# A two-layer decoder trunk: the low part of every second first-layer weight piece, on GpSimd or on VectorE

## The chip, the cores and the metric

The kernel runs on one core of one Trainium2 chip. The metric is the device time of one execution in microseconds (us); lower is better.

## What is computed

The input x is 512 x 1024 in float32. It passes two post-norm layers, each `x <- LayerNorm(alpha * x + sublayer(x))`. All arithmetic is meant in float32.

The first ("even") layer multiplies x by one wide input projection, whose columns feed two branches:

```python
proj = einsum('bsd,de->bse', x, w_in)      # q, k, v, g_ret, xb, g_lru, 1024 columns each
ret  = retention(rope(q), rope(k), v)      # 8 heads, decay per head, then a norm per head
ret  = ret * silu(g_ret)
lru  = rg_lru_branch(xb, ...) * silu(g_lru)   # width-4 convolution, two gates, a scan over time
y    = einsum('bse,ed->bsd', concatenate([ret, lru]), w_out)
```

The second ("odd") layer is differential attention with 8 heads, a gate path, and an output projection.

## The kernel before

**Numbers in two parts.** TensorE multiplies in a rounded 32-bit format (float32r). To keep float32 accuracy, every operand is kept as a pair: a high part, which is the operand rounded to float32r, and a low part, which is operand minus high part. A product is then three matrix products, high x high, high x low and low x high (`mm3`, lines 148 to 151). The pair is made by the helper `split` (line 139): ScalarE copies the source into the high part (line 145), and VectorE subtracts the high part from the source to give the low part (line 146). For weights that carry a scale, which occur only in the second layer, lines 142 and 143 do the same with a scale. Since `split` serves every operand, a row of the profile at L146 is told apart by its tile: `w59l` is the low part of weight piece 59, `k2l` the low part of head 2's rotated keys, `r53l` that of a block of retention scores, `retm3l` that of a finished retention branch, and so on. The letter h in place of l is the high part.

**Weight pieces.** The weights are cut on the host into pieces of 128 x 1024, in the order of their use, and numbered from 0 (list `order`). The pieces 0 to 63 belong to the first layer: 48 of its input projection and, mixed in where they are used, 16 of its output projection. From piece 64 on they belong to the second layer. `fetch` (line 163) brings the next piece: SyncE (SP) issues its DMA into a raw buffer (line 170), then `split` makes its two parts. There are two raw buffers, so the DMA of piece n+2 waits until both parts of piece n have been made. `take` (line 176) fetches so far ahead that mostly two pieces stand ready beyond the one in use.

**Order of the work.** TensorE and SP run in the order in which the program is written; for the other engines a scheduler orders the instructions by priority and by its own estimate of times, when the kernel is built. TensorE's order is a stream of projections (`t_unit`, `s_unit`, `out_unit`: 24 products of 512 columns for one weight piece) with side work between the products: class `Side` holds jobs (retention heads, recurrent channel blocks, attention blocks) that issue their next products after a given number of ticks of three products, written out by hand in the tables `RET_START`, `RET_SCORES`, `LRU_GATES` and so on. A side job's products can come only when VectorE and ScalarE have made their operands by then; otherwise TensorE waits.

**Lines that matter here.** In a retention head: rotation of q and k (lines 297 to 302), scores times decay (line 413, `rsd` from the PSUM tile `rs`), the products into `ro`, the square `rq` (line 424), its split, the mean by TensorE into `rv` (lines 430 and 431), and the norm (lines 435 to 445). In a recurrent block: the convolution `xc` in three VectorE steps (line 456), its split, the gates' products `pr` and `pi`, the steps at lines 472 to 484, whose last is the scan, and the product with the gate (line 487). The names that end in `_ps`, and `rs`, `ro`, `rv`, `pr`, `pi`, `ht`, are PSUM tiles; the others lie in SBUF. GpSimd works in the layer norm and in the second layer only, on one column at a time (`rsqrt`, lines 315 and 316, and line 591).

Of the kernel before, what the change touches and what calls it, by code (L numbers as in the profile page):

```python
# [8 lines left out]
F32 = mybir.dt.float32  # L9
F32R = mybir.dt.float32r  # L10
AF = mybir.ActivationFunctionType
ALU = mybir.AluOpType
# [11 lines left out]
LAMBDA_INIT = 0.8 - 0.6 * math.exp(-0.3)  # L24
MASKED = -3.0e38

# how many ticks the jobs' stages wait (see Side), by head, channel block or query block
RET_START = (13, 13, 13, 13, 13, 13, 13, 8)
RET_SCORES = (4, 4, 4, 7)
RET_NORM = (8, 6, 8, 6, 8, 6, 5, 5)  # L30
# [4 lines left out]
ATT_TURN = (4, 3, 4, 4)  # L35
ATT_NORM = 5
ATT_VALUE = 2
# how far the scheduler prefers these instructions to earlier ones
P_ROPE, P_SCORES, P_SQUARE, P_GROUP, P_VALUE = 50, 13, 60, 5, 60
P_CONV, P_GATES = 9, 5  # L40
P_LN, P_LAST, P_WEIGHTS, P_ATT = 10, 10, 450, 337
# [2 lines left out]


class Side:
    """Work that runs between the projections' products: jobs are generators that yield how many
    ticks (three products of 512 columns) have to pass before their next products are issued, or
    a condition for that."""

    def __init__(self):
        self.jobs = []
# [1 line left out]
        self.free = {}  # L54

    def add(self, gen, group, limit, wait=0, gap=0):
        """At most ``limit`` jobs of a group run at once, and they start ``gap`` ticks apart."""
        job = {"gen": gen, "at": self.now + wait, "group": group, "limit": limit, "gap": gap, "when": None, "started": False, "done": False}
        self.jobs.append(job)
        return job  # L60
# [35 lines left out]
def trunk(ctx: ExitStack, tc: tile.TileContext, a):  # L96
    nc = tc.nc
# [21 lines left out]
    ALL = slice(None)  # L119
# [4 lines left out]
    def temp(name):  # L124
        return es.tile([P, S], F32, tag="es", name=name)

    def bank(pl, tag, name):
        return pl.tile([P, 512], F32, tag=tag, name=name)

    def pair(pl, shape, tag, name, **kw):  # L130
        return tuple(pl.tile(shape, F32R, tag=tag + x, name=name + x, **kw) for x in "hl")

    def part(n, name):
        return pair(sp, [P, n], f"s{n}", name, bufs=2 if n == S else 1)

    def cut(t, *ix):
        return t[0][ix], t[1][ix]

    def split(src, dst, scale=None):
        if scale is not None:  # L140
            s = sg[:, scale:scale + 1]
            nc.scalar.activation(out=dst[0], in_=src, func=AF.Identity, scale=s)
            nc.vector.scalar_tensor_tensor(out=dst[1], in0=src, scalar=s, in1=dst[0].bitcast(F32), op0=ALU.mult, op1=ALU.subtract)
            return
        nc.scalar.copy(out=dst[0], in_=src)  # L145
        nc.vector.tensor_tensor(out=dst[1], in0=src, in1=dst[0].bitcast(F32), op=ALU.subtract)  # L146

    def mm3(out, l, r, start, stop):
        nc.tensor.matmul(out=out, lhsT=l[0], rhs=r[0], start=start, stop=False)  # L149
        nc.tensor.matmul(out=out, lhsT=l[0], rhs=r[1], start=False, stop=False)  # L150
        nc.tensor.matmul(out=out, lhsT=l[1], rhs=r[0], start=False, stop=stop)  # L151
# [3 lines left out]
        nc.sync.dma_start(out=t, in_=src)  # L155
        return t

    # ------------------------------------------------------------------ the weights' pieces, in the order of their use
    ew, ow, eo, oo = a["ev_w"], a["od_w"], a["ev_wo"], a["od_wo"]
    order, ready = [], []  # L160
    extra, stats = {}, {}

    def fetch():
        if len(ready) < len(order):
            n = len(ready)
            src, scale = order[n]
            raw = wraw.tile([P, D], F32, tag="raw", name=f"w{n}_r")
            w = pair(extra.pop(n, wsp), [P, D], "w", f"w{n}")
            for c in ([slice(0, HALF), slice(HALF, D)] if n == 0 else [slice(0, D)]):
                nc.sync.dma_start(out=raw[:, c], in_=src[:, c])  # L170
                split(raw[:, c], cut(w, ALL, c), scale=scale)
            ready.append(w)

    taken = [0]
# [69 lines left out]
    for p in range(3):  # L244
        one, two = (2 * p, 2 * p + 1)
# [5 lines left out]
    for kind, i in ev:  # L251
        if kind in ("ro", "lo", "out"):
            order += [(eo[2 * i + j + n], None) for n in {"ro": (0,), "lo": (8,), "out": (8, 0)}[kind] for j in range(2)]
        else:
            n = 4 if kind == "v" else 1
# [20 lines left out]
    ones = const.tile([P, P], F32R, tag="ones", name="ones")  # L276
# [60 lines left out]
        return [[load(f"{name}{r}{hf}", [P, HALF], src[r:r + 1, hf * HALF:hf * HALF + HALF].partition_broadcast(P), *next(slots))  # L337
                 for hf in range(2)] for r in range(2)]

    # ------------------------------------------------------------------ even layer  # L340
    phase = ctx.enter_context(ExitStack())
    es = pool("es", 10, phase)
    qkp = pool("qkp", 2, phase)
# [1 line left out]
    y = big.tile([P, SB, D], F32, tag="y", name="y")  # L345
# [10 lines left out]
    cos = load("cos", [P, S], a["cos"])  # L356
    sin = load("sin", [P, S], a["sin"])

    # 4 * softplus(-lambda), softplus(z) = max(z, 0) + log1p(exp(-|z|)), log1p(y) = 2 atanh(y / (2 + y))
    sp4 = const.tile([P, KT], F32, tag="sp4", name="sp4")  # L360
    sa = const.tile([P, KT], F32, tag="sa", name="sa")
    sb_ = const.tile([P, KT], F32, tag="sb_", name="sb_")
# [1 line left out]
    lam = vecs[:, 7]  # L364
# [40 lines left out]
    def retention(h, q, k, v, dec, m):  # L405
        ss = []
        for jb in range(SB):
            n = S - jb * P
            ps = bank(ps_sc, "sc", f"rs{h}{jb}")
            mm3(ps[:, :n], cut(k, ALL, slice(jb * P, jb * P + P)), cut(q, ALL, slice(jb * P, S)), True, True)  # L410
            with tc.high_priority(P_SCORES):
                s = temp(f"rsd{h}{jb}")
                nc.vector.tensor_tensor(out=s[:, :n], in0=ps[:, :n], in1=dec[:, :n], op=ALU.mult)  # L413
                t = part(n, f"r{h}{jb}")
                split(s[:, :n], t)
            ss.append(t)
            yield RET_SCORES[jb]
        ps = bank(ps_av, "av", f"ro{h}")
        hs = (h % 4) * P
        for jb in range(SB):  # L420
            mm3(ps[:, jb * P:], cut(v[jb], ALL, slice(hs, hs + P)), ss[jb], jb == 0, jb == SB - 1)
        with tc.high_priority(P_SQUARE):
            sq = temp(f"rq{h}")
            nc.scalar.activation(out=sq, in_=ps, func=AF.Square)
            t = part(S, f"rq{h}")
            split(sq, t)
        seen.add(h)
        yield RET_NORM[h]
        pv = bank(ps_tp, "tp", f"rv{h}")
        nc.tensor.matmul(out=pv, lhsT=ones, rhs=t[0], start=True, stop=False)  # L430
        nc.tensor.matmul(out=pv, lhsT=ones, rhs=t[1], start=False, stop=True)
        with tc.high_priority(P_GROUP):
            sd = temp(f"rsd{h}")
            # one Newton step makes r = exp(-ln(var + eps) / 2) exact: (r r (var + eps) - 3) r = -2 / sqrt(var + eps)
            nc.scalar.activation(out=sq, in_=pv, func=AF.Ln, bias=epsb)
            nc.scalar.activation(out=sd, in_=sq, func=AF.Exp, scale=-0.5)
            nc.scalar.activation(out=sq, in_=sd, func=AF.Square)
            nc.vector.scalar_tensor_tensor(out=sq, in0=pv, scalar=EPS, in1=sq, op0=ALU.add, op1=ALU.mult)
            nc.vector.scalar_tensor_tensor(out=sd, in0=sq, scalar=3.0, in1=sd, op0=ALU.subtract, op1=ALU.mult)
            n1 = sq  # L440
            nc.vector.tensor_tensor(out=n1, in0=ps, in1=sd, op=ALU.mult)
            nc.vector.tensor_scalar(out=n1, in0=n1, scalar1=gng[:, h:h + 1], scalar2=gn[:, 1, h:h + 1], op0=ALU.mult, op1=ALU.add)
        if ("gr", h) not in gates:
            yield lambda: ("gr", h) in gates
        nc.vector.tensor_tensor(out=n1, in0=n1, in1=gates.pop(("gr", h)), op=ALU.mult)
        split(n1, cut(m, ALL, h % 2))

    def lru(c, ps, m):
# [15 lines left out]
        t = temp(f"t{c}")  # L464
# [2 lines left out]
        mm3(pi, cut(gw[0], ALL, slice(o + P, o + 2 * P)), t2, True, True)  # L467
        i = xb
        nc.scalar.activation(out=i, in_=pi, func=AF.Sigmoid, bias=gbx(c))  # L469
        # t = tanh(-log_a / 2): a = (1 - t) / (1 + t), sqrt(1 - a^2) = 2 sqrt(t) / (1 + t)  # L470
        nc.scalar.activation(out=t, in_=t, func=AF.Tanh, scale=sp4[:, c:c + 1])
        nc.vector.tensor_tensor(out=i, in0=i, in1=xc, op=ALU.mult)  # L472
        d = xc
        r = temp(f"r{c}")
        # d = -1 / (1 + t), by one Newton step from exp(-ln(1 + t))
        nc.scalar.activation(out=r, in_=t, func=AF.Ln, bias=1.0)
        nc.scalar.activation(out=r, in_=r, func=AF.Exp, scale=-1.0)  # L477
        nc.vector.scalar_tensor_tensor(out=d, in0=t, scalar=1.0, in1=r, op0=ALU.add, op1=ALU.mult)  # L478
# [28 lines left out]
    for kind, i in ev:  # L507
# [5 lines left out]
        elif kind == "xb":  # L513
            if i % 2 == 0:
                raw = load(f"gw{i}", [P, 4 * P], a["gw"][i // 2], pl=es, tag="es")
# [42 lines left out]
    hj = []  # L558
    even_out(("lru", "ret"), 3, "eo", after=even_end)

    # ------------------------------------------------------------------ odd layer
    phase.close()
    lq = load("lq", [P, 4, P], a["lq"].partition_broadcast(P), pl=wk, tag="wk")
    nc.vector.tensor_tensor(out=lq[:, 0:2], in0=lq[:, 0:2], in1=lq[:, 2:4], op=ALU.mult)
# [6 lines left out]
    def attention(hd, qb, q, k, m):  # L571
        hc = (hd % 2) * 2 * P
        n = (qb + 1) * P
        ee = []
        z = small.tile([P, 2], F32, tag="z", name="z")
# [8 lines left out]
                nc.scalar.activation(out=e, in_=ps[:, :n], func=AF.Exp, scale=-1.0, bias=nm, accum_out=z[:, mp:mp + 1])  # L584
            ee.append(e)
        with tc.high_priority(P_ATT):
            # e0 / z0 - lam e1 / z1 = (e0 - lam (z0 / z1) e1) / z0; the RMS norm takes the 1 / z0, its epsilon times z0^2
            zr = small.tile([P, 2], F32, tag="zr", name="zr")
            nc.vector.reciprocal(out=zr[:, 0:1], in_=z[:, 1:2])  # L589
            nc.vector.tensor_scalar(out=zr[:, 0:1], in0=zr[:, 0:1], scalar1=z[:, 0:1], scalar2=nlam, op0=ALU.mult, op1=ALU.mult)  # L590
            nc.gpsimd.tensor_scalar(out=zr[:, 1:2], in0=z[:, 0:1], scalar1=z[:, 0:1], scalar2=EPS, op0=ALU.mult, op1=ALU.mult)  # L591
            nc.vector.scalar_tensor_tensor(out=ee[0], in0=ee[1], scalar=zr[:, 0:1], in1=ee[0], op0=ALU.mult, op1=ALU.add)  # L592
# [171 lines left out]
```

## Time and profile before

| | before |
|---|---|
| three runs | 947.27, 947.78, 945.7 us |
| median | 947.27 us |
| span of the profiled execution, first to last instruction | 944.1 us |
| mean granted TensorE clock | 0.994 |
| busy: TensorE / VectorE / ScalarE / GpSimd | 924.1 / 692.6 / 462.2 / 55.7 us |

The profiled execution is known by its span alone; the median of the runs is 3.2 us over it. In the profile PE is TensorE's products, PEld its weight loads, DVE is VectorE, ACT is ScalarE, POOL is GpSimd, SP or SPq is SyncE's queue of DMA issues. A row of the timeline has start, length, engine, line, operation, output<-inputs and shape; in square brackets behind it stands how long the engine had been idle before and what ended that. A row of the waits has who waited for whom, the total, the number of times and the longest. A row of the groups ends in busy time, mean ns of one, and the idle time ahead of it. In the busy times by stage each engine has its busy time and its number of instructions.

### The profile page before, as it was taken

How to read it: one execution, taken by the hardware profiler on the slowest of the kernel's cores; microseconds unless marked ns; L12 is line 12 of the kernel's file. 1: busy time of each engine (PE TensorE's matmuls, PEld its weight loads, DVE VectorE, ACT ScalarE, POOL GpSimd, SP SyncE). 2: the span in 40 equal slices, each digit the busy share in tenths (PEclk: the TensorE clock that was granted, in tenths of full speed). 3: DMA queues.
4: the chain of work that ended last, by engine and by line, in shares of the span. 5: the costliest groups of instructions: out<-in, count | busy, mean ns of one | idle time of the engine just before them, and what ended most of it. 6: DMA issues, size and time to landing. Idle time of an engine off the chain costs nothing.

```text
span 944.1 us, 11558 instructions
## 1 busy us (share of the span) xinstructions
PE 924.1 (98%) x4327; PEld 764.1 (81%) x4327; DVE 692.6 (73%) x1171; ACT 462.2 (49%) x749; POOL 55.7 (6%) x117
## 2 busy tenths in 40 slices
PE   8999999999999999999999999999999999999995
PEld 6888888878888888888887888888788888887884
DVE  6777997867869988994489854478844488636687
ACT  5567786566374776423334454233453234444330
POOL 0000000000000000000001210100100001101012
PEclk9999999999999999999999999999999999999998
DMA  6462221412414123305221122042222141223102
GB/s 225 156 215 87 69 88 56 166 58 69 143 33 167 57 90 115 123 18 173 90 89 68 67 90 90 23 134 90 68 70 86 45 134 67 85 79 114 57 23 90
DMA packets 27416, 88.94 MB, mean 94 GB/s; under 512 B 3424, under 2 KB 3552, under 8 KB 27360
## 3 DMA queue, kind: packets, MB, share of 16 engines
q1 hardware_dynamic: 27360, 88.20, 27.8%
q8 instruction: 34, 0.56, 0.2%
q14 instruction: 22, 0.18, 0.1%
HBM read 86.09 MB, written 2.10 MB: 93 GB/s over the span
## 4 chain that ended last, share of the span: by engine, by line
PE 74%; DVE 13%; ACT 5%; issue 3%; POOL 2%; DMA 1%; SPq 0%; POOLq 0%; DVEq 0%; ACTq 0%
PE ov_ps L151 3%; PE ov_ps L149 3%; PE ov_ps L150 3%; PE og_ps L149 3%; PE og_ps L150 2%; PE og_ps L151 2%; PE oo_ps L149 2%; PE oo_ps L150 2%; PE oo_ps L151 2%; PE ev_ps L149 2%; PE ev_ps L151 2%; PE ev_ps L150 2%; PE xb_ps L151 1%; PE xb_ps L150 1%; PE xb_ps L149 1%
## 5 line engine op out<-in xcount | busy, mean ns | idle before, releaser
L584 ACT ACTIVATE e<-as,nm 128x128 f32<-128x128 f32 (+3 forms) x64 | 33.2, 523 | 29.1 <-DVE nm L581 28.8
L615 DVE SCALAR_TENSOR_TENSOR o<-po,ars,og 128x256 f32<-128x256 f32 x32 | 15.5, 483 | 39.9 <-POOL ars L316 39.9
L581 DVE CUSTOM_DVE_ANT_0 as<-as,mask 128x128 f32<-128x128 f32 (+3 forms) x64 | 30.1, 509 | 1.9 <-PE as L151 1.9
L591 POOL TENSOR_SCALAR zr<-z 128x1 f32<-128x1 f32 x32 | 11.2, 351 | 309.1 <-ACT e L584 309.1
L315 POOL TENSOR_SCALAR rs_t<-bmv 128x1 f32<-128x1 f32 x8 | 3.8, 469 | 430.2 <-DVE bmv L326 430.2
L611 ACT ACTIVATE po<-po 128x256 f32<-128x256 f32 x32 | 11.9, 371 | 29.8 <-PE po L151 29.8
L315 POOL TENSOR_SCALAR rs_t<-ss,zr 128x1 f32<-128x1 f32 x32 | 15.9, 496 | 140.7 <-ACT po L611 135.7
L456 DVE SCALAR_TENSOR_TENSOR xc<-xbp,vecs,xc 128x509 f32<-128x509 f32 (+2 forms) x24 | 17.8, 743 | 2.1 <-ACT xc L453 1.9
L234 DVE TENSOR_TENSOR y<-oo_ps,y 128x512 f32<-128x512 f32 x24 | 16.2, 683 | 4.2 <-PE oo_ps L151 4.2
L316 POOL TENSOR_TENSOR ars<-rs_t,nhalf 128x1 f32<-128x1 f32 x32 | 18.9, 590 | 2.7
L592 DVE SCALAR_TENSOR_TENSOR e<-e,zr,e 128x128 f32<-128x128 f32 (+3 forms) x32 | 17.6, 550 | 1.0
L589 DVE RECIPROCAL zr<-z 128x1 f32<-128x1 f32 x32 | 5.2, 162 | 15.1 <-ACT e L584 14.9
L413 DVE TENSOR_TENSOR rsd<-rs,dec 128x512 f32<-128x512 f32 (+3 forms) x32 | 15.4, 483 | 0.8 <-PE rs L151 0.7
L620 PEld LDWEIGHTS po<-ident,o 128*128 128x128 f32 x64 | 8.4, 140 | 7.7 <-DVE o L615 4.5
L620 PE MATMUL po<-ident,o 128*128 128x128 f32 x64 | 12.6, 278 | 1.5 <-DVE o L615 1.3
L596 PE MATMUL wt<-ident,e 128*128 128x128 f32 x80 | 14.0, 273 | 0.0
L596 PEld LDWEIGHTS wt<-ident,e 128*128 128x128 f32 x80 | 10.4, 140 | 3.9 <-DVE e L592 0.4
L145 ACT CAST hh<-ht 128x512 fp32r<-128x512 f32 x8 | 4.7, 588 | 17.5 <-PE ht L551 17.5
L472 DVE TENSOR_TENSOR xbp<-xbp,xc 128x512 f32<-128x512 f32 x8 | 5.5, 690 | 10.0 <-ACT xbp L469 10.0
L584 ACT ACTIVATION_READ_ACCUMULATOR e<-as,nm 128x1 f32 x64 | 12.5, 196 | 0.0
L382 ACT ACT_TABLE_LOAD x9 | 11.5, 1283 | 1.5 <-PE gl_ps L151 1.4
L478 DVE SCALAR_TENSOR_TENSOR xc<-t,r 128x512 f32<-128x512 f32 x8 | 5.5, 690 | 9.0 <-ACT r L477 9.0
(2665 smaller groups left out, 3409.9 us busy)
## 6 DMA issues: line engine op xcount, KB each, us to landing
w_r<-in_od_w SPq DMA_DIRECT2D x64, 512.0 KB, 3.3
w_r<-in_ev_w SPq DMA_DIRECT2D x47, 512.0 KB, 3.3
w_r<-in_ev_wo SPq DMA_DIRECT2D x16, 512.0 KB, 3.4
w_r<-in_od_wo SPq DMA_DIRECT2D x16, 512.0 KB, 3.3
dec<-in_dec SPq DMA_DIRECT2D x8, 256.0 KB, 3.8
y<-in_x SPq DMA_DIRECT2D x4, 512.0 KB, 6.8
out_h<-y SPq DMA_DIRECT2D x8, 256.0 KB, 2.1
xr<-in_xt SPq DMA_DIRECT2D x3, 512.0 KB, 6.7
```

The costliest lines, as they stand in the source:

```text
L149: nc.tensor.matmul(out=out, lhsT=l[0], rhs=r[0], start=start, stop=False)
L150: nc.tensor.matmul(out=out, lhsT=l[0], rhs=r[1], start=False, stop=False)
L151: nc.tensor.matmul(out=out, lhsT=l[1], rhs=r[0], start=False, stop=stop)
L234: nc.vector.tensor_tensor(out=yy, in0=ps, in1=yy, op=ALU.add)
L315: nc.gpsimd.tensor_scalar(out=t, in0=var, scalar1=scale, scalar2=eps, op0=ALU.mult, op1=ALU.add)
L316: nc.gpsimd.tensor_tensor(out=out, in0=t, in1=nhalf[:, :1], op=ALU.pow)
L456: nc.vector.scalar_tensor_tensor(out=xc[:, sh:], in0=xb[:, :S - sh], scalar=conv_w(w, c), in1=xc[:, sh:], op0=ALU.mult, op1=ALU.add)
L581: nc.vector.tensor_tensor_reduce(out=ps[:, :n], in0=ps[:, :n], in1=mask[:, S - n:], scale=-QK_SCALE, scalar=3.0e38, op0=ALU.add, op1=ALU.m ...
L584: nc.scalar.activation(out=e, in_=ps[:, :n], func=AF.Exp, scale=-1.0, bias=nm, accum_out=z[:, mp:mp + 1])
L592: nc.vector.scalar_tensor_tensor(out=ee[0], in0=ee[1], scalar=zr[:, 0:1], in1=ee[0], op0=ALU.mult, op1=ALU.add)
L596: nc.tensor.transpose(out=pt[:, kb * P:kb * P + P], in_=ee[0][:, kb * P:kb * P + P], identity=ident)
L620: nc.tensor.transpose(out=pm[:, i * P:i * P + P], in_=o[:, i * P:i * P + P], identity=ident)
```

## The change

`split` gets one more argument, the engine that makes the low part; its default is VectorE. `fetch` passes GpSimd for the pieces with an odd number from 5 to 65, and VectorE for all others. (Pieces with a scale do not look at the argument; none of them is below 66.) The high parts stay on ScalarE, the transfers on SP. The subtraction itself, with its two inputs and its result, is the same.

```diff
-    def split(src, dst, scale=None):
+    def split(src, dst, scale=None, low=nc.vector):
         if scale is not None:
...
         nc.scalar.copy(out=dst[0], in_=src)
-        nc.vector.tensor_tensor(out=dst[1], in0=src, in1=dst[0].bitcast(F32), op=ALU.subtract)
+        low.tensor_tensor(out=dst[1], in0=src, in1=dst[0].bitcast(F32), op=ALU.subtract)
...
                 nc.sync.dma_start(out=raw[:, c], in_=src[:, c])
-                split(raw[:, c], cut(w, ALL, c), scale=scale)
+                split(raw[:, c], cut(w, ALL, c), scale=scale, low=nc.gpsimd if n % 2 and 3 < n < 66 else nc.vector)
```

Beside this the diff only takes comments out; line numbers stay.

## The prediction

> **What bounds the kernel now.** I read the page first, then the busy time by stage, then who waits for whom on TensorE, then the timeline around each of those waits. Times are microseconds.
>
> ```profile
> span 944.1 us, 11558 instructions
> PE 924.1 (98%) x4327; PEld 764.1 (81%) x4327; DVE 692.6 (73%) x1171; ACT 462.2 (49%) x749; POOL 55.7 (6%) x117
> ```
>
> The whole kernel is a TensorE stream: 924.1 of 944.1. VectorE, with 73%, is no bound as an average. The change touches the first layer alone, so that stage is what counts. In the view by stage the columns are PE, PEld, DVE, ACT, POOL busy time (with counts), then granted clock and DMA.
>
> ```profile
> 26.00:386.00 360.00, 357.87 (x1620) 296.25 (x1619) 296.42 (x440) 236.03 (x310) 0.00 (x0) 1.00 0.31 105
> ```
>
> From 26 to 386 TensorE is idle for only 360 - 357.9 = 2.1, at granted clock 1.00. VectorE is busy for 296.4 of 360 (82%) and GpSimd for nothing. So there is almost nothing to win here, and 64 of VectorE time lie free. What could be won is in the waits of TensorE in this stage:
>
> ```profile
> PE pi L149 <- DVE rsd L413: 0.5, 1, 0.5
> PE ro L150 <- DVE r31l L146: 0.5, 1, 0.5
> PE rv L430 <- ACT rq7h L145: 0.3, 1, 0.3
> PE rs L149 <- DVE rsd L413: 0.3, 1, 0.3
> PE rv L431 <- DVE rq1l L146: 0.2, 1, 0.2
> PE rv L431 <- DVE rq7l L146: 0.2, 1, 0.2
> PE ro L150 <- DVE r53l L146: 0.2, 1, 0.2
> ```
>
> They sum to 2.2. None of them names a weight piece: TensorE waits for VectorE's side work (retention and the gates), at seven places where that work arrives with no room. A gain cannot be much over 2.2; a loss has no such bound.
>
> **The change, part by part.** It moves the low part of the odd pieces 5 to 65, (65 - 5)/2 + 1 = 31 instructions, from VectorE to GpSimd. Their rows on VectorE, first and last of the 31:
>
> ```profile
> L146 DVE TENSOR_TENSOR w5l<-w_r,w5h 128x1024 fp32r<-128x1024 f32 x1 | 1.2, 1216 | 0.0
> L146 DVE TENSOR_TENSOR w65l<-w_r,w65h 128x1024 fp32r<-128x1024 f32 x1 | 1.2, 1206 | 0.0
> ```
>
> *Removed:* 31 x 1.21 = 37.5 of VectorE time. It lies under TensorE's stream, so it is worth only what it does for the seven waits.
>
> *Added:* 31 GpSimd subtractions of 128x1024. No row shows one. Below nothing is excluded for the instruction itself: it has the same two inputs and result. The nearest rows are VectorE's own, 1.2, as the lower end, and one-column instructions on both engines for the upper:
>
> ```profile
> L316 POOL TENSOR_TENSOR ars<-rs_t,nhalf 128x1 f32<-128x1 f32 x32 | 18.9, 590 | 2.7
> L589 DVE RECIPROCAL zr<-z 128x1 f32<-128x1 f32 x32 | 5.2, 162 | 15.1 <-ACT e L584 14.9
> ```
>
> 590/162 = 3.6, and 3.6 x 1.21 = 4.4 is the upper end. I take 2.4, twice VectorE's row: the low end of one-column ratios is fixed cost, which a thousand columns spread out, so the value should lie nearer to 1.2 than to 4.4. The Trainium skill (GPSIMD Engine Reference, section Performance versus the Vector engine) gives 4497 ns against 2293 ns for a fp32 add of 2048 columns, which would make 2.25 here, an estimate; no run here shows it.
>
> *Does GpSimd disturb VectorE?* The trace has GpSimd instructions beside VectorE's in the second layer:
>
> ```profile
> 516.19 0.27 POOL L315 TENSOR_SCALAR rs_t<-ss,zr 128x1 f32<-128x1 f32 x1 [1.59 <-ACT po L611]
> 516.20 0.68 DVE L301 TENSOR_TENSOR q20o_s<-q20o_ps,sin 64x512 f32<-64x512 f32 x1
> 524.74 0.68 DVE L302 TENSOR_TENSOR q21o_c<-q21o_c,q21o_s 128x512 f32<-128x512 f32 x1
> 525.16 1.44 POOL L315 TENSOR_SCALAR rs_t<-ss,zr 128x1 f32<-128x1 f32 x1 [2.65 <-ACT po L611]
> 525.34 1.22 DVE L146 TENSOR_TENSOR w86l<-w_r,w86h 128x1024 fp32r<-128x1024 f32 x1
> ```
>
> The same one-column instruction takes 0.27 beside a VectorE instruction with a PSUM input, and 1.44 beside two in a row whose inputs both lie in SBUF; it ends at 526.60, just after the second one (526.56). So one of them has to be over before the other goes on. I take it that this holds both ways: a GpSimd subtraction that has started keeps back VectorE's next instruction with two SBUF inputs for its whole 2.4. No row of before shows that direction, since GpSimd's instructions here read one column. The Trainium skill (SBUF — State Buffer, section Who interferes with whom) states both directions: a VectorE instruction with two SBUF inputs and a GpSimd instruction that reads SBUF share a read interface, and the one that issues second is fully blocked. By that rule the sum is the one that follows; without the reverse direction it is the first rival's.
>
> If each of the 31 holds VectorE for its full length, VectorE loses 31 x 2.4 = 74 and saves 37.5: net 37 in a stage with 64 free. It does not become the bound as a whole; what counts is the places with little room.
>
> *Place A, near 136.* The high part of piece 23 ends at 131.60, while VectorE runs two-input work up to 133.22; then comes one with a PSUM input and GpSimd can start.
>
> ```profile
> 130.57 1.03 ACT L145 CAST w23h<-w_r 128x1024 fp32r<-128x1024 f32 x1
> 132.00 1.22 DVE L484 TENSOR_TENSOR_SCAN xc<-t,r 128x512 f32<-128x512 f32 x1
> 133.72 0.68 DVE L487 TENSOR_TENSOR xc<-xc,gl 128x512 f32<-128x512 f32 x1
> 134.32 0.68 DVE L146 TENSOR_TENSOR k2l<-k_c,k2h 128x512 fp32r<-128x512 f32 x1
> 136.07 0.40 PE L151 MATMUL rs<-q2h,k2l 128*128 128x512 f32 x1
> ```
>
> 133.22 + 2.4 = 135.62: L487 moves by 1.90, k2l ends at 136.90 in place of 135.00, and TensorE wants it at 136.07: **+0.8** (0 with 1.2, +2.8 with 4.4).
>
> *Place B, near 320.* The high part of piece 53 ends at 315.10, with a PSUM-input instruction on VectorE. GpSimd starts there, to 317.5, and keeps back L478, the head of a chain (in the view of the last-ending chain) that runs through VectorE and ScalarE to a wait of TensorE:
>
> ```profile
> 314.06 1.04 ACT L145 CAST w53h<-w_r 128x1024 fp32r<-128x1024 f32 x1
> 315.20 0.69 DVE xc L478
> ...
> 320.69 0.33 PE ro L150
> ```
>
> **+2.3** (+1.1 to +4.3).
>
> *Place E, near 307.* The high part of piece 51 ends at 299.38; VectorE's convolution (three two-input steps) heads a chain without a gap to the 0.5 wait of pi:
>
> ```profile
> 298.33 1.05 ACT L145 CAST w51h<-w_r 128x1024 fp32r<-128x1024 f32 x1
> 300.64 0.70 DVE xc L456
> ...
> 307.58 0.50 PE pi L149
> ```
>
> 299.4 + 2.4 = 301.8 against 300.6: **+1.2** (-0.5, the wait itself, if pieces 47 and 49 off VectorE let it run ahead; up to +3.2).
>
> *Place D, near 391.* Piece 63 is the weight with the least room:
>
> ```profile
> 386.78 1.05 ACT L145 CAST w63h<-w_r 128x1024 fp32r<-128x1024 f32 x1 [3.74 <-PE ro_ps L151]
> 387.79 0.68 DVE L445 TENSOR_TENSOR rq<-rq,gr 128x512 f32<-128x512 f32 x1
> 390.12 0.68 DVE L146 TENSOR_TENSOR retm3l<-rq,retm3h 128x512 fp32r<-128x512 f32 x1
> 390.88 0.39 PE L150 MATMUL eo_ps<-w63l,retm3h 128*128 128x512 f32 x1
> 391.11 0.39 PE L151 MATMUL eo_ps<-w63h,retm3l 128*128 128x512 f32 x1
> ```
>
> GpSimd starts when L445 ends, 388.47, and is done at 390.87: piece 63 is just in time, but retm3l starts at 390.87, ends at 391.55 and is wanted at 391.11: **+0.5** (0 to +2.5).
>
> *Place C, near 377: a gain.* A raw buffer comes free only with the low part, and the transfer two pieces on waits for it. Piece 59's low part stood in VectorE's queue long after its high part, so piece 61 landed late, and ScalarE sat idle in front of it, with the square rq (L424), whose TensorE input was ready, behind it in its queue:
>
> ```profile
> 359.39 1.04 ACT L145 CAST w59h<-w_r 128x1024 fp32r<-128x1024 f32 x1
> 367.85 1.22 DVE L146 TENSOR_TENSOR w59l<-w_r,w59h 128x1024 fp32r<-128x1024 f32 x1
> 374.40 1.05 ACT L145 CAST w61h<-w_r 128x1024 fp32r<-128x1024 f32 x1 [5.63 <-DMA w_r<-in_ev_wo]
> ```
>
> GpSimd's queue is empty: 360.43 + a wait of 0.4 + 2.4 = 363.2 in place of 369.07. Piece 61 comes some 6 earlier, rq too, and the two waits of rv on rq7h and rq7l (0.3 + 0.2) go: **-0.5**.
>
> *At nothing:* the other weights, since a subtraction that starts behind its high part is done about as early as VectorE's, which stood in a queue; SP's queue, whose transfers wait for GpSimd in place of VectorE; and GpSimd's own queue, empty until 386. If the subtraction took 4.4, that cover would still leave only piece 63 late (by 2).
>
> **Sum:** 0.8 + 2.3 + 1.2 + 0.5 - 0.5 = +4.3: a span of 944.1 + 4.3 = 948.4. The median of the runs is 947.27, 3.2 over the span; with the same 4.3 it becomes 951.6. VectorE's order is drawn up anew by the scheduler, so the places may move; their kind should not.
>
> **The rivals.** *1. GpSimd yields and never holds VectorE.* For it: only that direction is in the rows. Against: whichever comes second should wait. Then A, B and D cost nothing, C and part of E are won: -0.5 - 0.5, 946.3. *2. The subtraction is long (4.4).* For: GpSimd's 590 ns for one column. Against: that is fixed cost. The upper ends: A 2.8, B 4.3, E 3.2, D 2.5, less 0.5: +12, 959. It decides from 2.4 on, where piece 63 starts to be late. *3. Faster: the queue in front of VectorE is what made the seven waits.* As at C, odd pieces no longer stand in line, transfers start earlier and ScalarE stops sitting in front of them. If all seven waits go, -2.2: 945.1. For: the 7.4 between w59h's end and w59l's start. Against: rq1l and r31l have no odd piece close ahead of them, so not all can go; and it needs a GpSimd that hardly holds VectorE. *4. Nothing moves:* holding and relief cancel, or the new order hides both: 947.3.
>
> **How the numbers follow.** A difference under 0.2% (1.9) can't be told from no change here; the three runs of before lie 2.1 apart. Forecast 0.42, of which 0.05 within 0.2% (a subtraction near 1.2 makes A, D and E nothing: +1.1 - 0.5). Rival 1 0.25, of which 0.05 faster by more; rival 2 0.10; rival 3 0.13, faster; rival 4 0.10. Slower 0.37 + 0.10 = 0.47; same 0.05 + 0.20 + 0.10 = 0.35; faster 0.05 + 0.13 = 0.18. Both signs hold much of it: the forecast's own range is 948 to 956. The whole range is 945.3 to 957, leaving out the best of rival 3 and the worst of rival 2.
>
> **What would show it.** On GpSimd 31 rows of 128x1024 with an undisturbed length near 2.4; VectorE's two-input instructions starting late or lasting longer right behind them, those with PSUM inputs not; TensorE's waits in the first layer up from 2.2 to 6 or 7, on VectorE and not on a weight; ScalarE's 5.6 before w61h gone. Two-input rows of VectorE at 0.68 inside a GpSimd subtraction would make the forecast wrong and rival 1 right; waits of TensorE for GpSimd would speak for rival 2.

## The result and the profile after

| | before | after |
|---|---|---|
| median of 4 runs | 947.52 us (945.7 to 948.27) | 972.96 us (972.89 to 973.02) |
| span of the profiled execution | 944.1 us | 971.2 us |
| waits of TensorE, 26 to 450 | 424 - 421.87 = 2.1 us | 424 - 406.14 = 17.9 us |
| VectorE busy | 692.6 us | 700.4 us |

The ratio is 1.0275, with a 95% interval of 1.0263 to 1.0287: slower by 25.4 us, where 4.3 were forecast. The two spans differ by 27.1: the profiled execution of before is near the fastest of its four runs. First the page of the kernel after: the head, and three groups of VectorE.

```profile
span 971.2 us, 11603 instructions
PE 935.0 (96%) x4327; PEld 767.7 (79%) x4327; DVE 700.4 (72%) x1140; ACT 462.1 (48%) x749; POOL 134.3 (14%) x148
...
L456 DVE SCALAR_TENSOR_TENSOR xc<-xbp,vecs,xc 128x509 f32<-128x509 f32 (+2 forms) x24 | 22.2, 925 | 6.1 <-ACT xc L453 5.7
L484 DVE TENSOR_TENSOR_SCAN xc<-t,r 128x512 f32<-128x512 f32 x8 | 11.9, 1492 | 0.1
L413 DVE TENSOR_TENSOR rsd<-rs,dec 128x512 f32<-128x512 f32 (+3 forms) x32 | 15.2, 481 | 3.0 <-PE rs L151 3.0
```

VectorE has 31 instructions fewer (1171 to 1140), 31 x 1.21 = 37.5 of work less, and yet is busy for 7.8 more. What came back are longer rows: laid side by side, instruction by instruction, those of the first layer grew by 42 in all, in 27 rows. (Neighbouring rows overlap a little in the profile, so the busy time does not follow from 42 - 37.5: without the 31 subtractions, in a kernel further down, VectorE is busy for 660.8, and the longer rows make up the 39.6 from there to 700.4.) The groups say which: the convolution (L456), whose inputs all lie in SBUF, takes 925 ns in the mean (743 before), the scan (L484) 1492 (1217 before); the product with the decay (L413), which reads PSUM, is as short as it was (483 before).

The timeline shows it instruction by instruction, at two of the 31 subtractions (columns: start, length, engine, line):

```profile
136.75 0.68 DVE L302 TENSOR_TENSOR k_c<-k_c,k_s 128x512 f32<-128x512 f32 x1
137.03 2.67 POOL L146 TENSOR_TENSOR w23l<-w_r,w23h 128x1024 fp32r<-128x1024 f32 x1 [13.71 <-ACT w23h L145]
137.35 3.42 DVE L484 TENSOR_TENSOR_SCAN xc<-t,r 128x512 f32<-128x512 f32 x1
...
380.63 2.57 POOL L146 TENSOR_TENSOR w59l<-w_r,w59h 128x1024 fp32r<-128x1024 f32 x1 [18.00 <-ACT w59h L145]
380.86 0.69 DVE L413 TENSOR_TENSOR rsd<-rs,dec 128x512 f32<-128x512 f32 x1
381.46 2.30 DVE L483 TENSOR_TENSOR r<-r,xbp 128x512 f32<-128x512 f32 x1
```

The scan, 1.22 before, takes 3.42: it is held until GpSimd is done at 137.03 + 2.67 = 139.70, and about its own length is left behind that. At 381 the instruction with a PSUM input passes beside the subtraction at 0.69; the next, with two SBUF inputs, takes 2.30. And w23l got in between k_c and the scan, which stood ready behind it: GpSimd waits for the running instruction alone, not for the run of them. Of the 31 subtractions 27 held one row of VectorE each, by 0.33 to 2.21, in the mean 1.5; four (pieces 11, 33, 39 and 57) held none.

The waits of TensorE in the first layer (who, for whom, total, times, longest):

```profile
PE pi L149 <- DVE rsd L413: 4.0, 2, 2.5
PE rs L149 <- DVE rsd L413: 2.5, 3, 1.5
PE rv L430 <- ACT rq7h L145: 2.1, 1, 2.1
PE rs L149 <- ACT k4h L145: 1.5, 1, 1.5
PE rv L431 <- DVE rq7l L146: 1.3, 1, 1.3
PE pr L149 <- ACT xc2h L145: 1.1, 1, 1.1
PE rs L151 <- DVE k2l L146: 1.1, 1, 1.1
PE pr L149 <- ACT xc6h L145: 1.0, 1, 1.0
PE ro L150 <- DVE r53l L146: 1.0, 1, 1.0
PE ro L149 <- ACT r53h L145: 0.7, 1, 0.7
```

The rows are the largest ones. Before, the longest was 0.5 and all made 2.2. None of these names a weight piece or GpSimd. Where ScalarE is named (k4h, xc2h, xc6h, rq7h, r53h) it copies what VectorE has just finished: the delay comes through it. The busy times by stage (PE, PEld, DVE, ACT, POOL, granted clock, DMA) show a second effect, after the two longest waits:

```profile
320.00:328.00 8.00, 5.84 (x15) 4.68 (x16) 5.45 (x9) 4.75 (x7) 0.00 (x0) 0.59 0.01 2
399.50:407.00 7.50, 6.16 (x15) 4.65 (x16) 5.28 (x6) 6.19 (x8) 1.10 (x1) 0.54 0.56 175
```

The granted clock falls to 0.59 and 0.54 there, in stretches of 6.8 each; before it was 1.00 all through this stage. When the same products of TensorE in the two traces are laid side by side, the kernel after is late by 1.3 from the start, ahead of any moved piece (at the start TensorE ran at half clock for 6.8, in the profiled execution of before for 3.4); by the end of the first layer it is late by 26.7, and at the very end by 27.1. The second layer took no part in it.

### The profile page after: what moved, and what is told of

The parts are those of the page before. It is cut to its first block, busy times and chain, and to the rows that moved or that the text cites. A ratio compares the mean times of both kernels' runs of the same rounds, so it can differ in the third digit from the quotient of the medians.

```text
span 971.2 us, 11603 instructions
## 1 busy us (share of the span) xinstructions
PE 935.0 (96%) x4327; PEld 767.7 (79%) x4327; DVE 700.4 (72%) x1140; ACT 462.1 (48%) x749; POOL 134.3 (14%) x148
## 4 chain that ended last, share of the span: by engine, by line
PE 54%; DVE 24%; ACT 11%; issue 5%; POOL 3%; DMA 2%; SPq 0%; POOLq 0%; DVEq 0%; ACTq 0%
PE ov_ps L151 3%; PE ov_ps L150 3%; PE ov_ps L149 3%; PE og_ps L149 2%; PE og_ps L150 2%; PE og_ps L151 2%; PE oo_ps L149 2%; PE oo_ps L150 2%; PE oo_ps L151 2%; DVE xc L456 1%; ACT e L584 1%; DVE xc L484 1%; DMA w_r<-in_ev_wo 1%; POOL rs_t L315 1%; POOL ars L316 1%
## 5 line engine op out<-in xcount | busy, mean ns | idle before, releaser
L591 POOL TENSOR_SCALAR zr<-z 128x1 f32<-128x1 f32 x32 | 11.3, 352 | 308.2 <-ACT e L584 308.2
L456 DVE SCALAR_TENSOR_TENSOR xc<-xbp,vecs,xc 128x509 f32<-128x509 f32 (+2 forms) x24 | 22.2, 925 | 6.1 <-ACT xc L453 5.7
L413 DVE TENSOR_TENSOR rsd<-rs,dec 128x512 f32<-128x512 f32 (+3 forms) x32 | 15.2, 481 | 3.0 <-PE rs L151 3.0
L596 PEld LDWEIGHTS wt<-ident,e 128*128 128x128 f32 x80 | 10.4, 140 | 3.9 <-DVE e L592 0.4
L332 DVE SCALAR_TENSOR_TENSOR y<-y,lrs,ln 128x512 f32<-128x512 f32 x16 | 11.4, 746 | 2.2 <-POOL lrs L316 2.2
L484 DVE TENSOR_TENSOR_SCAN xc<-t,r 128x512 f32<-128x512 f32 x8 | 11.9, 1492 | 0.1
```

The costliest lines, as they stand in the source:

```text
L456: nc.vector.scalar_tensor_tensor(out=xc[:, sh:], in0=xb[:, :S - sh], scalar=conv_w(w, c), in1=xc[:, sh:], op0=ALU.mult, op1=ALU.add)
L484: nc.vector.tensor_tensor_scan(out=d, data0=t, data1=r, initial=0.0, op0=ALU.mult, op1=ALU.add)
L596: nc.tensor.transpose(out=pt[:, kb * P:kb * P + P], in_=ee[0][:, kb * P:kb * P + P], identity=ident)
```

## The experiments

The theory was now: GpSimd's subtraction holds VectorE's SBUF-to-SBUF instructions, and each hold is passed on to TensorE wherever little room is left. The rivals: the new order that the scheduler gave VectorE and ScalarE; the length of one hold, which shorter pieces would mend; the subtraction's place; and the clock. Each kernel is compared with runs of before made beside it, whose median moves between 946.86 and 947.52. In the diffs, `low=...` stands for the change's own choice in `fetch`, and `piece` is called for the odd pieces 5 to 65.

### The hold without a new order

All low parts are made on VectorE, as before, and GpSimd makes beside it a subtraction of 960 columns for 30 pieces, which nobody reads.

```diff
+                split(raw[:, c], cut(w, ALL, c), scale=scale)
...
+    if n % 2 and 3 < n < 64:
+        t = extra["spare"].tile([P, 960], F32R, tag="spare", name="spare")
+        nc.gpsimd.tensor_tensor(out=t, in0=raw[:, :960], in1=w[0][:, :960].bitcast(F32), op=ALU.subtract)
```

> VectorE makes all low parts again, in the order of the kernel before, and GpSimd makes those of the odd pieces 5 to 63 a second time into a spare tile (960 of 1024 columns) that nobody reads. Hold theory (a GpSimd subtraction keeps back VectorE's SBUF-to-SBUF instructions for its whole length, and TensorE waits where that work has no room): VectorE's rows grow by about 40 us as in the changed kernel, with none of the 37 us saved, so it is at least as slow as the changed kernel: 972 to 995 us. Order theory (the loss comes from the new order of VectorE and ScalarE): within 3 us of the kernel before, 945 to 950 us.

Measured: 992.61 against 946.86, ratio 1.0478 (1.0463 to 1.0494), +45.7. VectorE and ScalarE ran their instructions in exactly the order of before. Its largest waits and the stage:

```profile
PE rs L149 <- ACT k4h L145: 5.3, 1, 5.3
PE rs L149 <- DVE rsd L413: 3.0, 3, 1.5
PE pr L149 <- ACT xc2h L145: 2.6, 1, 2.6
PE pi L149 <- DVE rsd L413: 2.5, 1, 2.5
```

```profile
26.00:450.00 424.00, 394.21 (x1699) 319.23 (x1698) 357.99 (x464) 241.77 (x316) 88.58 (x32) 0.96 0.28 93
```

All four stand in the kernel after too, k4h and xc2h with less (1.5 and 1.1), and no order has changed: the loss does not need a new order. The 45.7 is not the hold alone. TensorE runs at half clock for 30.7 of this stage (13.7 in the kernel after). And the raw buffer is now read by both engines and comes free later: for the pieces 5 to 63 ScalarE stands 49.4 in front of a weight's transfer, against 27.8 before and 32.7 in the kernel after.

Late transfers are thus a rival too. In the kernel after, the chain of work was followed back from each wait of TensorE that is over 0.5: each time it meets a row of VectorE that a subtraction holds, and only in front of rq7h does it pass a weight's transfer on the way there (place C below).

### The relief without the hold

The odd pieces get no low part; the product with the low part uses the high part. This leaves 31 subtractions out.

```diff
+def piece(nc, raw, w):
+    nc.scalar.copy(out=w[0], in_=raw)
+    return w[0], w[0]
```

> The low part of the odd pieces 5 to 65 is not made at all, and their products take the high part in its place: TensorE does the same work, VectorE is relieved of 37 us, and GpSimd does nothing. Both theories give the worth of the relief alone. Hold theory: the relief is worth at most the 2.2 us of waits plus what the starts of products show as lost, so 943 to 947.5 us. Order theory: here too the order of VectorE is drawn up anew, so a loss of 5 us or more could show: 950 to 973 us.

Measured: 946.77 against 946.86, ratio 0.9999 (0.999 to 1.0008).

```profile
26.00:450.00 424.00, 421.56 (x1915) 349.02 (x1914) 311.28 (x478) 256.20 (x336) 7.06 (x8) 1.00 0.31 104
```

VectorE's busy time in this stage falls from 343.6 to 311.3 and TensorE's stays (421.87 before, 421.56 here). VectorE's order was drawn up anew here too (61 of its rows would have to move to give the order of before, 44 in the kernel after), so a new order as such need not cost anything. And the relief, free of any price, is worth nothing: there was nothing to win by taking work off VectorE, whoever took it.

### The port by itself

A kernel that doesn't compute the reference at all: VectorE repeats one kind of instruction of 512 columns while GpSimd subtracts 1024.

```diff
+            nc.gpsimd.tensor_tensor(out=q, in0=g, in1=x[:, 3], op=ALU.subtract)
...
+            nc.vector.tensor_tensor(out=o, in0=va, in1=x[:, 2, :S], op=ALU.subtract)
```

> Not the reference's computation: a small kernel that copies x to the output and runs ten VectorE instructions of 512 columns beside two GpSimd instructions of 1024 columns, stage by stage; VectorE's are two SBUF inputs (alone; beside subtractions; beside memsets), one PSUM and one SBUF input, a tensor_scalar SBUF to SBUF, a reduction from SBUF; last GpSimd alone with 1024, and with 64 to 768 columns. Hold theory: beside subtractions one or two rows of VectorE with two SBUF inputs, and of tensor_scalar, last 2 to 3 us longer or the subtraction does; PSUM-input rows, reductions and rows beside memsets keep their length within 0.05 us. If it is a sharing of bandwidth and no hold, every row beside a subtraction is longer by a like share. GpSimd alone: 2.4 us for 1024 columns, about 1.25 for 512 and 0.7 for 256.

Measured, by groups (busy time, mean ns of one): the first row is VectorE alone, the next four are instructions of VectorE beside a subtraction, the last three are GpSimd alone.

```profile
L41 DVE TENSOR_TENSOR o<-va,x 128x512 f32<-128x512 f32 x9 | 5.5, 686 | 2.9 <-DMA x<-in_x 2.9
...
L41 DVE TENSOR_TENSOR o<-va,x 128x512 f32<-128x512 f32 x1 | 2.2, 2223 | 0.0
L43 DVE TENSOR_TENSOR o<-pt,x 128x512 f32<-128x512 f32 x3 | 1.9, 676 | 0.0
L45 DVE TENSOR_SCALAR o<-va 128x512 f32<-128x512 f32 x2 | 4.9, 2500 | 0.0
L47 DVE TENSOR_REDUCE o<-va 128x1 f32<-128x512 f32 x7 | 4.2, 678 | 0.0
...
L61 POOL TENSOR_TENSOR q<-g,x 128x1024 f32<-128x1024 f32 x2 | 4.9, 2454 | 10.0 <-ACT g L54 10.0
L67 POOL TENSOR_TENSOR q<-g,x 128x512 f32<-128x512 f32 x1 | 1.3, 1260 | 0.1
L67 POOL TENSOR_TENSOR q<-g,x 128x256 f32<-128x256 f32 x1 | 0.7, 722 | 0.1
```

Two SBUF inputs: 2.22 in place of 0.69. A PSUM input (L43) and a reduction (L47): not touched. One SBUF input and an SBUF result (L45), 0.41 alone, is held as well, 2.50; the prediction had counted the two-input kind alone. The held rows are 1.5 to 2.1 longer, where 2 to 3 had been expected. The Trainium skill (SBUF — State Buffer, section Who interferes with whom) states that the port pair which the two engines share is locked for one of them at a time; these rows agree for a VectorE instruction that comes second. For the other direction there is w23l above: it began while k_c ran and took 2.67, where most of the 31 took 2.40. The part of this kernel that was to show GpSimd only writing did not bring the two side by side, so that is left open.

### Shorter holds

Each subtraction in four of 256 columns, all on GpSimd.

```diff
+    for j in range(4):
+        e = slice(j * 256, j * 256 + 256)
+        nc.gpsimd.tensor_tensor(out=w[1][:, e], in0=raw[:, e], in1=w[0][:, e].bitcast(F32), op=ALU.subtract)
```

> As the changed kernel, but each GpSimd subtraction is cut into four of 256 columns, so that VectorE can come in between; VectorE and ScalarE run in the order of the changed kernel. Hold theory: one hold is about 0.7 us in place of 2.4, few places have less room, so most of the 25 us are gone: 947 to 957 us. Order theory: 970 to 976 us, as the changed kernel. If GpSimd gets in again ahead of the waiting VectorE instruction each time, the four act as one: also about 973 us, and then the rows of VectorE would show one long extension.

Measured: 975.98, ratio 1.0305 (1.0288 to 1.0322). The expectation for a hold (947 to 957) failed: not better than the change itself. The time lies where the new order as the cause had been put (970 to 976), but the two experiments above speak against that. The timeline at the first place:

```profile
137.58 5.00 POOL L770 TENSOR_TENSOR w23l<-w_r,w23h 128x256 fp32r<-128x256 f32 x4 [11.94 <-ACT w23h L767]
137.91 1.76 DVE L484 TENSOR_TENSOR_SCAN xc<-t,r 128x512 f32<-128x512 f32 x1
...
255.59 1.04 ACT L767 CAST w41h<-w_r 128x1024 fp32r<-128x1024 f32 x1 [3.47 <-DMA w_r<-in_ev_wo]
```

A single hold is now short (the scan takes 1.76, not 3.42), and over the stage VectorE's rows grow by 23 in place of 42. But the two engines take turns, a whole low part takes 3.8 in the mean in place of 2.43, the raw buffer comes free later, and the next transfer with it: ScalarE stands 3.47 in front of w41h, with k4h behind it, and TensorE's wait for k4h is 3.8 here (1.5 in the kernel after). At this place what a shorter hold saves, the longer occupation of the buffer takes back; that it is so at the other places was not followed.

A variant that does less on GpSimd: it makes 512 columns of each odd piece, VectorE the other 512.

```diff
+    for e, low in ((slice(0, HALF), nc.gpsimd), (slice(HALF, D), nc.vector)):
+        low.tensor_tensor(out=w[1][:, e], in0=raw[:, e], in1=w[0][:, e].bitcast(F32), op=ALU.subtract)
```

> For each of the 31 pieces GpSimd makes only the left 512 columns of the low part, VectorE the right 512. The small kernel had a GpSimd subtraction of 512 columns at 1.26 us in place of 2.34. Hold theory: the waits in the changed kernel (17.9 us in 16 jumps at nine chains) each fall by about 1.1, to some 7.6 in all, and the waits of over 2 us that came before half clock are gone or nearly: 954 to 959 us. If, as with the four quarters, a shorter hold is no better because the low part as a whole is done no earlier and VectorE has its own half in line beside GpSimd's: 967 to 976 us.

Measured: 959.71, ratio 1.0133 (1.0116 to 1.015): +12.8, half of the loss for half the columns, just above the 954 to 959 that the hold had been given. The sum of VectorE's lengthened rows is about 14, a third.

### Which pieces cost

Going back along the chain from each wait of the kernel after, I found nine pieces whose subtraction held the head of it. One kernel moves these nine only, one the other 22, one the three of the prediction's places A, E and B, and one nine behind whose subtraction I had found no wait.

```diff
-... low=nc.gpsimd if n % 2 and 3 < n < 66 else nc.vector)
+... low=nc.gpsimd if n in (15, 19, 23, 25, 41, 51, 53, 59, 61) else nc.vector)
...
+... low=nc.gpsimd if n in (23, 51, 53) else nc.vector)
...
+... low=nc.gpsimd if n in (5, 9, 11, 27, 29, 31, 33, 35, 43) else nc.vector)
```

> Only nine of the 31 pieces are moved to GpSimd: 15, 19, 23, 25, 41, 51, 53, 59, 61, those whose subtraction, in the changed kernel, holds a VectorE instruction that stands in a chain to a wait of TensorE. Place theory (a hold costs what the chain behind it lacks in room, and nothing elsewhere): the waits of those nine chains sum to 17.9 us in the changed kernel and two stretches at half clock add about 5, so 962 to 971 us. Load theory (every moved piece costs VectorE the same, 25.4/31 = 0.82 us): 9 x 0.82 = 7.4, 953 to 956 us.

> The other 22 odd pieces are moved to GpSimd, the nine stay on VectorE. Place theory: 946 to 952 us, a little over the kernel before at most, as the order is drawn up anew and some hold may meet a chain that it missed. Load theory: 22 x 0.82 = 18, 962 to 967 us.

> Only the pieces 23, 51 and 53 are moved to GpSimd, the three whose holds the prediction had as places A, E and B. Place theory with the waits of the changed kernel: A 1.2, E 1.2 to 2, B 1.8, so +4.2 to +5 us, 951 to 952.5 us. Prediction's own terms: 0.8 + 1.2 + 2.3 = 4.3, 951.3 us. Load theory: 3 x 0.82 = 2.5, 949.5 us.

> Nine other pieces are moved, 5, 9, 11, 27, 29, 31, 33, 35 and 43, behind whose holds the changed kernel's trace shows no wait of TensorE. Place theory: 946 to 948.5 us. Load theory: 9 x 0.82 = 7.4, 953.5 to 955 us.

| pieces moved | median (before) | ratio, 95% interval | us | us a piece |
|---|---|---|---|---|
| the nine | 962.38 (946.98) | 1.0164 (1.0145 to 1.0183) | +15.4 | 1.71 |
| the other 22 | 958.27 (946.98) | 1.0126 (1.0109 to 1.0142) | +11.3 | 0.51 |
| 23, 51, 53 | 953.44 (947.36) | 1.0062 (1.0046 to 1.0079) | +6.1 | 2.0 |
| nine without a wait | 950.43 (947.36) | 1.0032 (1.0021 to 1.0043) | +3.1 | 0.34 |

The place matters: the nine cost over three times as much a piece as the 22. But it does not decide alone, as I had expected it to: the 22 and even the nine "without a wait" cost something too, and both times lie between the range by place and the range by load. With other pieces moved, other chains are the late ones; in the last of these kernels TensorE waits for k4h, rsd and r53l (0.6, 0.6 and 0.5). Nine and 22 together make 26.7, close to the 25.4 of all 31. The kernel with three pieces carries the prediction's own terms:

```profile
PE pi L149 <- DVE rsd L413: 1.7, 1, 1.7
PE ro L149 <- ACT r53h L145: 1.1, 1, 1.1
PE rs L151 <- DVE k2l L146: 1.1, 1, 1.1
PE ro L150 <- DVE r53l L146: 1.0, 1, 1.0
```

Beside the trace of before, TensorE's products fall behind by 1.2 at A, 1.2 at E and 2.2 at B, together 4.6. The rest up to 6.1 is a stretch of 3.4 at half clock behind B's two waits (some 1.6), which no expectation had, so the time lies above all of them.

### The clock

First by itself: a kernel that doesn't compute the reference, in which TensorE makes 96 products again and again, with a wait for a chain of ScalarE copies of growing length between the blocks.

```diff
+        for j in range(96):
+            nc.tensor.matmul(out=b, lhsT=l, rhs=z, start=j == 0, stop=j == 95)
...
+            for j in range(k):
+                nc.scalar.copy(out=z, in_=src if j == 0 else src.bitcast(F32))
```

> Not the reference's computation: a small kernel that copies x to the output, and on TensorE runs nine stretches of 96 products of 512 columns (about 22 us each), between which TensorE waits for a chain of 1, 2, 3, 4, 5, 6, 1 ScalarE copies, some 0.9 to 5 us. Clock theory (a wait of TensorE of about 2 us or more is followed by a stretch at half clock, which costs about 2.5 to 3.4 us more): the copies 1 and 2 (up to about 1.6 us) leave the clock at 1.00, 4 to 6 (over 2.5 us) are followed by 3.4 or 6.8 us at 0.50, and 3 is at the edge. Rival (the half clock in the changed kernel has another cause, such as the number of waits): no half clock after the start, whatever the wait.

Measured, in the timeline (the length of a block, and in brackets the wait ahead of it):

```profile
127.63 22.08 PE L37 MATMUL b<-z,l 128*128 128x512 f32 x96 [2.62 <-ACT z L42]
152.98 23.67 PE L37 MATMUL b<-z,l 128*128 128x512 f32 x96 [3.27 <-ACT z L42]
180.57 23.60 PE L37 MATMUL b<-z,l 128*128 128x512 f32 x96 [3.92 <-ACT z L42]
```

Up to 2.62 a wait costs nothing beyond itself, and from 3.27 the block is 1.6 longer. (2.62 had been expected to lose the clock.) The Trainium skill (TensorE: Matmul & The Clock Gate, section What's actually happening) says that the clock falls after an idle window of about 3.4 us; these blocks come near that, with 2.62 kept and 3.27 lost. The kernel after does not: it lost the clock after one wait of 2.47 (pi), with 1.04 and 0.23 in the 4 us ahead of it, and after 2.06 and 1.34 with work between (rv). The three-piece kernel lost it after 1.10 and 1.01. So it takes less than one such wait when waits lie close together. Nor do the lengths alone decide: near 120 the kernel after waited 1.15 and 0.54 for xc2 and kept the clock, and the next kernel waited 1.10 and 0.54 there and lost it. What does decide is not settled here.

Then in the kernel after: TensorE gets 7 products into a spare PSUM bank ahead of that pi, and 7 and 4 ahead of the two products into rv, to keep it at work while it waits.

```diff
+        c == 6 and fill(nc, bank(ps_pj, "pj", "fill"), ones, 7)
...
+    for _ in range(n):
+        nc.tensor.matmul(out=d, lhsT=ones, rhs=ones.unsqueeze(1).to_broadcast([P, 4, P]), start=True, stop=True)
```

> The changed kernel with dummy products of 512 columns on TensorE in front of the three products that waited longest (7 before pi of block 6, 7 and 4 before the two of rv of head 7), written to a spare PSUM bank that nobody reads. They lie within the waits of 2.47, 2.06 and 1.34 us (7 take about 1.6, 4 about 0.9). Clock theory (the two stretches of 6.8 us at half clock come from these waits, and cost about 2.4 us each): they go, and the time falls by 4 to 5.5 us, to 967.5 to 969 us. Rival (the half clock costs nothing beside the waits, or comes from something else): 971.5 to 975 us.

Measured: 976.34, ratio 1.0312 (1.0296 to 1.0329), 3.4 slower than the kernel after and above both expected ranges. The same two stretches, one at half clock that the kernel after did not have, and the waits that came for it:

```profile
121.00:124.40 3.40, 3.40 (x9) 2.66 (x10) 2.66 (x3) 2.66 (x5) 2.15 (x1) 0.50 0.48 164
320.00:328.00 8.00, 7.15 (x33) 5.60 (x32) 5.92 (x10) 6.09 (x9) 0.00 (x0) 1.00 0.01 2
399.50:407.00 7.50, 6.77 (x28) 4.82 (x27) 5.56 (x8) 4.07 (x6) 1.91 (x1) 1.00 0.55 175
```

```profile
PE eo_ps L150 <- POOL w63l L146: 1.9, 1, 1.9
PE ro L149 <- ACT r53h L145: 1.3, 1, 1.3
```

The clock is back at 1.00 in the two stretches, and TensorE gains 2.8 and 2.6 there on the kernel after. It loses that again: to the new stretches at half clock near 121 and 339, of 3.4 each, and to longer waits for r53h and for the low part of piece 63. VectorE and ScalarE had another order here too, so this kernel is no clean undoing of one thing. It shows that full clock at these two places did not shorten the whole; how much the half clock adds to the total stays open.

## Why the prediction was wrong

By the lateness of TensorE's products, place for place, forecast and trace (times of the trace of before):

| place | forecast | measured |
|---|---|---|
| A, k2l, near 136 | +0.8 | +1.2 |
| E, block 6, near 307 | +1.2 | +3.9 |
| B, r53, near 320 | +2.3 | +1.8 |
| D, retm3l, near 391 | +0.5 | 0 |
| C, rq7, near 377 | -0.5 | +3.1 |
| near 83, 115, 142, 247 and 366 | not seen | 1.7 + 2.1 + 0.8 + 1.6 + 1.6 = 7.8 |
| half clock, twice | not seen | 2.5 + 2.3 = 4.8 |
| from the start; small steps | not seen | 1.3 + 2.8 |
| sum | +4.3 | +26.7 |

**What held.** The subtraction was taken at 2.4; the mean of 31 is 2.43, from 2.36 to 2.67. That is partly luck, since the rows of before left everything from 1.2 to 4.4 open. The hold works in the direction that no row of before showed, so rival 1 falls. PSUM inputs pass. TensorE never waits for a weight, so rival 2, a long subtraction, is not what made the loss. A, E and B, moved alone, make TensorE 4.6 late where 0.8 + 1.2 + 2.3 = 4.3 were forecast. And the relief is worth nothing, as the seven small waits said; rivals 3 and 4 fall with that.

**"What counts is the places with little room": this step failed, in how it was counted.** I took the seven waits of before for the list of such places. A wait shows where room is below zero; a place with room of 0.5 shows no wait and still loses 1.9 of a hold of 2.4. The gates near 83 and 115, and the scores of heads 2, 4 and 7 near 142, 247 and 366, are such places: 7.8 of the loss. And each place was given one hold. At E three fall on one run of VectorE's work, of the pieces 47, 49 and 51 (GpSimd at 296.16, 303.11 and 312.96). The rows held are the low part gw6l, q_c and the convolution, 0.69, 0.69 and 2.32 long before:

```profile
296.63 2.48 DVE L146 TENSOR_TENSOR gw6l<-gw,gw6h 128x512 fp32r<-128x512 f32 x1 [1.41 <-ACT gw6h L145]
303.49 2.56 DVE L302 TENSOR_TENSOR q_c<-q_c,q_s 128x512 f32<-128x512 f32 x1
314.09 3.39 DVE L456 SCALAR_TENSOR_TENSOR xc<-xbp,vecs,xc 128x509 f32<-128x509 f32 x3 [1.42 <-ACT xc L453]
```

Beside the trace of before, VectorE is late by 10.4 ahead of them and by 12.0, 13.5 and 14.6 behind the first, the second and the third; TensorE's 3.9 follow from that, over even the upper bound of 3.2. The prediction had hoped that 47 and 49 off VectorE would let it run ahead. Where the 22 pieces moved, with 47 and 49 among them and 51 not, TensorE's wait for this pi was still 2.5.

**Place A's working failed though its number was near.** GpSimd was to wait until VectorE's run of two-input work was over. It waits for one instruction, so a subtraction finds its gap at once and holds the next instruction of the kind that can be held: at A the scan (3.42), not L487. That this gave 1.2 beside the forecast 0.8 is luck. The 64 of free VectorE time were no protection; 27 of the 31 held a row.

**Place C had the wrong sign.** The step "the transfer two pieces on waits for it" took piece 59's late low part for what held up piece 61. The transfer stood in SP's queue, which is in order, behind the four loads of layer-norm parameters (L155). In the kernel after:

```profile
378.91 12.08 SPq L155 DMA_DIRECT2D ln<-in_ev_ln  x4
391.08 0.85 SPq L170 DMA_DIRECT2D w_r<-in_ev_wo  x2
...
397.12 1.04 ACT L145 CAST w61h<-w_r 128x1024 fp32r<-128x1024 f32 x1 [6.61 <-DMA w_r<-in_ev_wo]
398.25 2.36 POOL L146 TENSOR_TENSOR w61l<-w_r,w61h 128x1024 fp32r<-128x1024 f32 x1 [15.04 <-ACT w61h L145]
399.35 1.80 DVE L146 TENSOR_TENSOR rq7l<-rq,rq7h 128x512 fp32r<-128x512 f32 x1 [7.13 <-ACT rq7h L145]
```

These loads take 12.08 to issue (10.46 before), in which SP's queue waits 10.4 for VectorE's `rsd` (8.7 before). Piece 59's low part is done at 383.20, and piece 61 is issued only at 391.08; ScalarE's wait in front of w61h did not go but grew, from 5.63 to 6.61. The kernel without low parts shows the 10.46 of before on these four loads, though its piece 59 had no low part to wait for. Behind that, piece 61's own subtraction holds rq7l, the last row, and TensorE waits for rq7h and rq7l by 2.1 + 1.3.

**Two terms were not in the sum at all.** VectorE's one-input instructions on SBUF are held too: 5 of the 42 by which rows grew. And a wait of TensorE can cost more than itself through the granted clock, 4.8 in the trace, of which the filled kernel leaves open how much is added to the total.

**The range** ended at 957 since it left out the worst of rival 2. It had no case for "the same mechanism, at more places", which the count of 31 holds should have called for: 31 x 2.4 = 74 of holding at most (42 were measured) against 2.2 of known waits.

## What to carry to other kernels

Before work goes from VectorE to GpSimd in a stage that TensorE bounds, price it by VectorE's chains: here 27 of 31 such GpSimd instructions held a VectorE instruction, for 1.5 in the mean and up to 2.2, at once and not where VectorE is free, in exchange for 1.2 of work moved. Measure first what the relief is worth, by leaving the work out (here: nothing). And list every place by its room, not by its waits: a stage whose waits are near zero is the one in which any delay shows.

## What the runs showed of the hardware

- GpSimd gets its turn after the one VectorE instruction that runs, even when the next one is ready: the scan went from 1.22 to 3.42. Cut into four, the two engines alternate.
- VectorE instructions with one SBUF input and an SBUF result are held like those with two (0.41 to 2.50). A reduction (0.68) and a two-input instruction with one input in PSUM (0.68) were not, and none of the 27 held rows of the kernel after reads PSUM.
- GpSimd's float32 subtraction took 0.72, 1.26 and 2.45 for 256, 512 and 1024 columns: about 2.2 ns a column, and little beside that.
- TensorE's clock halved after a single wait of 3.27 but not of 2.62, and in the full kernels after shorter ones close together (1.10 and 1.01). Waits of nearly the same lengths (1.15 and 0.54, 1.10 and 0.54) kept it in one kernel and lost it in another.
